# One more 1024-row block of output columns 256 to 511 transposed before it is normalised, in a fused matmul and batch norm

## The chip, the core and the metric

The kernel runs on one core of a Trainium2 chip. The metric is the device time of one execution in microseconds (us). A profile shows one execution: its span runs from the first to the last instruction, and the device time is a little longer than that. All times of events below are counted in us from the start of the span.

## The reference

```python
y = np.matmul(x, weight)                     # x: 16 x 512 x 1024, weight: 1024 x 768, float32
mean = np.mean(y, axis=(0, 1), keepdims=True)
var = np.var(y, axis=(0, 1), keepdims=True)
y_norm = (y - mean) / np.sqrt(var + eps)
return gamma * y_norm + beta                 # 8192 x 768 float32, 25.17 MB
```

The statistics of a column run over all 8192 rows, so no element of a column can be finished before the last product of that column is known. After that, the rest is one multiplication by a scale and one addition of a shift for each column.

## The kernel before, in words

The 8192 rows are 16 chunks of 512 (C = 16). The 768 columns are six tiles of 128 (nt = 0 to 5). x comes in through POOL's DMA queue with a cast to bf16, DVE transposes it, and TensorE (PE) multiplies.

**Two layouts.** Tiles 0 and 1 are computed with the rows of the output on the partitions ("in rows"; L500 to L516). They are finished by a DVE multiplication and an addition on POOL or DVE, and stored by L945. Tiles 2 to 5 are computed with the columns on the partitions ("in columns"; L562 to L584): scale and shift are then one number for each partition. ACT copies each finished PSUM bank to SBUF as bf16 (L714; tile 2 from chunk 4 on L719 and L723, which also sum), and DVE takes statistics (L710). Such a block has to be transposed before it is stored. A block is two chunks, 128x1024 (GY = 2), and its store is 512 KB.

**Three ways to finish a block in columns.** The tables MODE (L276) and RAW (L278) choose.
- "xact" (col_block, L1190): normalise in columns, on ACT for tile 2 (L1022) or on DVE for tile 3 (L1025); transpose by a DMA that SP issues (L1219); convert bf16 to float32 on ACT (L1231); store from SP (L1201).
- "pe" (the rest of tile 4): normalise, transpose on PE (L1043), copy out on ACT (L1209), store.
- "raw" (raw_turn, L1098, and raw_block, L1165): transpose the block by a DMA that SP issues, before any statistics are known, into a tile r_sb of the y pool (L1105). When scale and shift are known, raw_spread (L1126) lays them out along the free dimension (L1140 to L1157, in a PSUM bank). Then DVE multiplies (L1173, 128x1024), POOL adds (L1177), and SP stores (L1181).

Before the change tile 2 and tile 3 have blocks 0 and 2 raw (chunks 0, 1 and 2, 3), and their six other blocks "xact". Tile 4 has blocks 0, 2, 4, 6 raw.

**The order of the work.** Every operation is a Task with a due time, engines with costs, dependences and the memory slots it takes. arrange (L122) is a greedy planner: it goes through time and, on the engine that can begin first, places the ready task with the earliest due time (within 0.2 us). The resulting order on each engine is fixed in the program. A queue waits in order: an instruction whose input is late holds up everything behind it on its engine, SP included. Raw transposes of chunks 0 to 3 are entered with an early due time (L1121 to L1124); those of later chunks when all products of their tile are entered (L1275 to L1277). All raw transposes wait for the last load of x (gate, L1120). Of the raw blocks, raw_block number i (block 2i) is due at start + STEP * i + RAWDUE (L1284).

**Memory that the change touches.** The ring (RING, L279) is 6144 float32 words a partition. An "xact" block takes 1536 words of it when its transpose is issued (1024 until its store has landed); a raw block takes 1024 when its multiplication begins. The y pool has 29 tiles (YB). There are eight PSUM banks; the spread scale and shift of a tile hold one until its last raw block is multiplied.

**The tail.** Tile 5 is last. Its statistics close after the last product; then come a chain of small operations, DVE normalisation (L1347), PE transposes (L1043), ACT copies (L1360) and eleven stores (L1363). Before them one block of tile 4, held back for this, is stored (L1254).

Of the kernel before, what the change touches and what calls it, by code (L numbers as in the profile page):

```python
# [227 lines left out]
def kernel(  # L228
# [46 lines left out]
    PARTED, LATE, SINGLE = (4,5,7,8,9,10), (12,13,14,15), (2,3,6)  # L275
    MODE = {2:'xact',3:'xact',4:('pe',)*8}  # L276
    MODE = {nt: m if isinstance(m, tuple) else (m,) * (C // GY) for nt, m in MODE.items()}
    RAW, RAWADD, RAWDUE = {2:(0,2),3:(0,2),4:(0,2,4,6)}, {2:'POOL',3:'POOL',4:'POOL'}, {2:14.0,3:8.0,4:8.0}  # L278
    RING = 3 * CH // 32 * KQ // 2  # L279
    ENG = {"ACT": nc.scalar, "DVE": nc.vector, "POOL": nc.gpsimd, "SP": nc.sync}  # L280

# [1129 lines left out]
```

## Time and profile before

| | |
|---|---|
| time, median of 3 runs | 206.23 us (206.06 to 206.47) |
| the profiled execution: device time | 206.31 us |
| its span | 204.5 us |
| busy in the span: PE, DVE, ACT, POOL | 190.3, 159.2, 145.3, 128.3 us |
| HBM read, written | 36.71 MB, 25.17 MB |
| stores of blocks out of the ring, 512 KB | 37, 3.8 us to landing |
| transposes by DMA: "xact", raw | 12, 8 |

"Busy" counts the time in which an engine works on an instruction; a busy PE may still run matmuls that overlap. "To landing" is the time from the issue of a DMA to the arrival of its last byte. In the table by stretches, each engine has its busy time and, in brackets, the number of its instructions; then come the granted TensorE clock (1.00 is full), the busy share of the 16 DMA engines (packets of different queues overlap, so it goes over 1) and the GB/s that they moved.

### The profile page before, as it was taken

The numbers are of one execution on the slowest core, as the hardware profiler recorded it, in microseconds if no ns is written. First come the engines' busy times: TensorE is split into PE (matmuls) and PEld (weight loads), VectorE is DVE, ScalarE is ACT, GpSimd is POOL, SyncE is SP. The second block draws the span as 40 slices with busy tenths as digits, with TensorE's granted clock in tenths as the row PEclk, the third lists the DMA queues.
The fourth block names the chain that finished last, engine by engine and source line by source line (L and its number), as shares of the span: only waits on it lengthen the run. The fifth ranks groups of instructions, "written<-read, shape, count | busy, mean of one in ns | idle before, by whom it ended". The sixth has DMA issues, their size and how long they took to land.

```text
span 204.5 us, 3492 instructions
## 1 busy us (share of the span) xinstructions
PE 190.3 (93%) x1202; PEld 114.7 (56%) x1202; DVE 159.2 (78%) x248; ACT 145.3 (71%) x260; POOL 128.3 (63%) x152
## 2 busy tenths in 40 slices
PE   7999999999999999999999999999999999996800
PEld 3468555656588888777865444444444445445500
DVE  4031879999999999969988998977999787687700
ACT  2001361369989999998879766999998878936930
POOL 7877954877499989996303999389626402880000
PEclk9999999999999999999999999999999999999965
DMA  4999999999999999999599899999999999999996
GB/s 75 161 202 195 196 196 196 196 197 196 189 195 196 197 199 193 196 197 194 98 203 212 309 338 324 253 314 311 320 287 191 291 336 314 347 343 346 331 347 196
DMA packets 99602, 49.00 MB, mean 240 GB/s; under 512 B 25344, under 2 KB 99072, under 8 KB 99584
## 3 DMA queue, kind: packets, MB, share of 16 engines
q0 software_dynamic: 34624, 18.36, 65.2%
q1 hardware_dynamic: 64960, 30.42, 55.1%
q8 instruction: 9, 0.15, 0.3%
q14 instruction: 9, 0.07, 0.1%
HBM read 36.71 MB, written 25.17 MB: 303 GB/s over the span
## 4 chain that ended last, share of the span: by engine, by line
PE 76%; DMA 10%; ACT 4%; DVE 3%; POOL 2%; issue 1%; ACTq 0%; DVEq 0%; POOLq 0%
PE y_ps L574 49%; PE y_ps L509 21%; DMA w_sb<-in_weight_dram 6%; ACT o_sb L1360 3%; DMA ring<-in_x_dram 3%; PE y_ps L813 3%; DMA r_sb<-y_sb 1%; PE o_ps L1043 1%; POOL ring L402 1%; PE y_ps L752 1%; POOL w_sb L386 1%; DVE xT_sb L434 1%; DVE y_sb L1063 1%; ACTq L1406 0%; PE tot_ps L870 0%
## 5 line engine op out<-in xcount | busy, mean ns | idle before, releaser
L574 PEld LDWEIGHTS <-w_sb 128*128 128x128 bf16 x520 | 50.4, 97 | 57.4
L574 PE MATMUL y_ps<-xT_sb,w_sb 128*128 128x512 bf16 (+1 forms) x272 | 59.3, 371 | 0.0
L574 PE MATMUL y_ps<-x_pl,w_sb 128*128 128x512 bf16 x248 | 57.0, 379 | 0.0
L402 POOL DMA_DIRECT2D ring<-in_x_dram x76 | 47.3, 626 | 13.7 <-DVE xT_sb L427 5.0
L509 PE MATMUL y_ps<-w_sb,xT_sb 128*128 128x256 bf16 x448 | 50.5, 273 | 0.2 <-DVE xT_sb L434 0.2
L509 PEld LDWEIGHTS <-xT_sb 128*128 128x128 bf16 x448 | 43.7, 98 | 7.4 <-DVE xT_sb L434 0.8
L434 DVE STREAM_TRANSPOSE xT_sb<-ring 128x1024 f32<-128x1024 f32 (+1 forms) x29 | 31.2, 1111 | 13.3 <-DMA ring<-in_x_dram 13.2
L710 DVE BATCH_NORM_STATS2 stats<-y_ps 128x6 f32<-128x512 f32 x46 | 30.8, 686 | 6.8 <-PE y_ps L574 6.6
L546 ACT COPY x_pl<-xT_sb 128x1024 bf16<-128x1024 bf16 x34 | 34.8, 1059 | 1.7 <-DVE xT_sb L434 1.7
L714 ACT CAST y_sb<-y_ps 128x512 bf16<-128x512 f32 x51 | 28.5, 593 | 9.1 <-DVE stats L710 5.5
L941 POOL TENSOR_TENSOR ring<-ring,sum 128x1024 f32<-128x1024 f32 (+1 forms) x11 | 23.8, 2186 | 15.2 <-DVE ring L936 15.1
L658 ACT ACTIVATE sq_sb<-y_ps 128x512 f32<-128x512 f32 x28 | 16.5, 613 | 16.8 <-PE y_ps L509 16.4
L665 POOL TENSOR_TENSOR sum<-sum,sq_sb 128x512 f32<-128x512 f32 x20 | 25.5, 1276 | 3.4 <-ACT sq_sb L658 2.3
L661 DVE TENSOR_TENSOR sum<-y_ps,sum 128x512 f32<-128x512 f32 x28 | 18.9, 675 | 6.4 <-ACT sq_sb L658 5.4
L1177 POOL TENSOR_TENSOR ring<-ring,sum 128x1024 f32<-128x1024 f32 x8 | 19.5, 2448 | 5.7 <-issue 4.5
L671 ACT CAST y_sb<-y_ps 128x512 bf16<-128x512 f32 x28 | 16.0, 602 | 7.7 <-DVE sum L661 7.5
L936 DVE TENSOR_TENSOR ring<-y_sb,a_ps 128x1024 f32<-128x1024 bf16 (+1 forms) x16 | 16.7, 1079 | 0.3 <-DMA out_dram<-ring 0.3
L1144 POOL COPY sum<-sum 32x256 f32<-32x256 f32 (+1 forms) x17 | 5.3, 315 | 15.6 <-ACT sum L1144 8.8
L1231 ACT CAST ring<-ring 128x1024 f32<-128x1024 bf16 x12 | 12.7, 1060 | 2.3 <-DMA ring<-y_sb 2.3
L427 DVE STREAM_TRANSPOSE xT_sb<-ring 128x2048 bf16<-128x2048 bf16 x6 | 13.5, 2288 | 0.3 <-DMA ring<-in_x_dram 0.2
L1043 PE MATMUL o_ps<-ident,y_sb 128*128 128x128 bf16 x96 | 11.3, 221 | 1.6 <-DVE y_sb L1347 1.5
L590 PE MATMUL idle_ps<-idle_sb 128*128 128x512 f32 x18 | 11.2, 784 | 1.5 <-DVE idle_sb L316 1.5
(104 smaller groups left out, 152.4 us busy)
## 6 DMA issues: line engine op xcount, KB each, us to landing
out_dram<-ring SPq DMA_DIRECT2D x37, 512.0 KB, 3.8
ring<-in_x_dram POOLq DMA_DIRECT2D x52, 256.0 KB, 8.8
out_dram<-o_sb SPq DMA_DIRECT2D x6, 512.0 KB, 5.4
ring<-in_x_dram POOLq DMA_DIRECT2D x16, 128.0 KB, 6.0
w_sb<-in_weight_dram POOLq DMA_DIRECT2D x8, 192.0 KB, 6.1
out_dram<-ring SPq DMA_DIRECT2D x6, 256.0 KB, 3.6
ring<-in_x_dram POOLq DMA_DIRECT2D x4, 192.0 KB, 7.8
out_dram<-o_sb SPq DMA_DIRECT2D x3, 256.0 KB, 3.4
```

The costliest lines, as they stand in the source:

```text
L402: bi = seq(nc.gpsimd.dma_start(x_bf[32 * i:32 * i + 32], src[:, :, KQ * i:KQ * (i + 1)]))
L434: seq(nc.vector.transpose(dst, src[:, :, jw0:jw1]))
L509: seq(nc.tensor.matmul(y_ps[:, s], x_of(c, jw, e, t * P, (t + 1) * P), w_sb[:, jw, e, 0:NA], start=(s == 0 and jw == 0 and e == 0), stop=( ...
L546: seq(nc.scalar.copy(dst, pairs) if eng == "ACT" else ENG[eng].tensor_copy(dst, pairs))
L574: seq(nc.tensor.matmul(y_ps, w_sb[:, jw, e, nt * P:(nt + 1) * P], moving(c, jw, e, q0 * QR, q1 * QR, parted), start=(jw == 0 and e == 0 an ...
L661: seq(nc.vector.tensor_add(sum1, slot.tile[:, 0:n], sum1))
L665: seq(ENG[eng].tensor_add(acc, acc, state["sq"][:, 0:n]))
L710: seq(nc.vector.bn_stats(dst, slot.tile))
L714: seq(nc.scalar.copy(y(nt, c), slot.tile))
L936: seq(nc.vector.tensor_mul(slot.o, y_row[c].y[:, s0:s1], aff[0][:, None, :].to_broadcast([P, n, NA])))
L941: seq(ENG[eng].tensor_add(slot.o, slot.o, row[:, None, :].to_broadcast([P, n, NA])))
L1177: seq(ENG[eng].tensor_add(slot.o, slot.o, row[:, None, :].to_broadcast([P, n, P])))
```

## The change

Block 4 (chunks 4 and 5) of tile 2 and of tile 3 goes from "xact" to raw. Nothing else is edited; the planner arranges the whole program anew from the changed list of tasks.

```diff
-    RAW, RAWADD, RAWDUE = {2:(0,2),3:(0,2),4:(0,2,4,6)}, {2:'POOL',3:'POOL',4:'POOL'}, {2:14.0,3:8.0,4:8.0}
+    RAW, RAWADD, RAWDUE = {2:(0,2,4),3:(0,2,4),4:(0,2,4,6)}, {2:'POOL',3:'POOL',4:'POOL'}, {2:14.0,3:8.0,4:8.0}
```

## The prediction

> **What bounds the kernel now.** I read the waits of PE first, then the table by stretches, then SP's timeline and the landings of its stores.
>
> ```profile
> PE o_ps L1043 <- DVE y_sb L1347: 1.5, 1, 1.5
> PE idle_ps L590 <- DVE idle_sb L316: 1.5, 1, 1.5
> PE y_ps L509 <- DVE xT_sb L434: 0.2, 1, 0.2
> ```
>
> These are all of PE's waits: 1.5 us at the start, 0.2 us, and 1.5 us at the end, for the statistics of tile 5. From 110 to 186 PE never waits, and its starts follow each other at 0.216 or 0.226 us a matmul. So PE ends its last product at 186.15, and no edit that leaves the matmuls alone makes that earlier. The first store of tile 5 is issued at 188.85. What follows is 4.19 MB of stores.
>
> ```profile
> 116.00:136.00 20.00, 20.00 (x92) 8.67 (x91) 18.68 (x23) 16.32 (x39) 16.40 (x7) 1.00 0.90 292
> 136.00:152.00 16.00, 16.00 (x75) 7.20 (x74) 13.69 (x27) 15.96 (x24) 9.62 (x11) 1.00 1.15 323
> 152.00:160.00 8.00, 8.00 (x38) 3.60 (x37) 7.01 (x10) 6.16 (x9) 5.92 (x9) 1.00 1.25 193
> 160.00:173.00 13.00, 13.00 (x73) 6.29 (x71) 10.07 (x23) 11.44 (x22) 2.18 (x4) 1.00 1.19 327
> 173.00:186.00 13.00, 13.00 (x77) 6.84 (x76) 9.76 (x15) 8.38 (x13) 9.41 (x4) 1.00 1.15 344
> 186.00:190.00 4.00, 2.43 (x30) 1.55 (x28) 3.50 (x13) 3.15 (x9) 0.00 (x0) 1.00 1.15 346
> 190.00:204.50 14.50, 3.63 (x46) 2.47 (x44) 3.18 (x10) 6.21 (x8) 0.00 (x0) 0.69 0.96 289
> ```
>
> The last two columns are the reading. Stores alone run at 344 to 346 GB/s (173 to 190): that is a full queue, 1.51 us for a store of 512 KB. At 116 to 136 (292) and 152 to 160 (193) the queue is short of work or stuck; from 160 on it is full up to the end, but for a dip at 190 to 192 (308 GB/s). Look also at ACT: 15.96 of 16 us in 136 to 152. There ACT is what makes blocks ready.
>
> ```profile
> 180.40 5.01 SPq L1181 DMA_DIRECT2D out_dram<-ring  x3
> 187.07 1.04 SPq L1254 DMA_DIRECT2D out_dram<-ring  x2
> 188.85 11.01 SPq L1363 DMA_DIRECT2D out_dram<-o_sb  x11
> ```
>
> The last store of tile 4, issued at 184.34, lands at 190.00, the two of L1254 at 190.75 and 191.52, the first of tile 5 at 191.91, the last at 203.62. The landings follow each other at 1.51 us per 512 KB with no break, although the mean of the 16 engines dips at 190. So one engine is behind the others and stays so: after 202.3, where the rate breaks off, 34 or so packets of 27 ns follow, 0.92 us. The packet records show why that can be: an instruction fetch of 16 KB at 180.50 took 0.92 us. **The end is the backlog of the slowest DMA engine.** Were the queue empty when tile 5 comes, the end would be 0.9 us earlier and no more, because 188.85 is PE's.
>
> **The change, part by part.** For each of the two blocks:
>
> Removed. Tile 2: one normalisation on ACT (L1022, 1.25 us) and one conversion (L1231, 1.06): 2.31 us of ACT. Tile 3: one conversion, 1.06 us of ACT, and one DVE normalisation (L1025, 0.54). Two L1219 transposes, and 1536 words of ring each. ACT is full from 130 to 152, so there 2.31 us make the next blocks of tile 2 ready earlier: the first normalisation, at 127.24, is that of block 6 instead of 4, each later conversion comes one place sooner, and the last store of tile 2's columns (156.29) comes at about the place of the one before it (151.96).
>
> Added. Two DVE multiplications (L1173, 1.22 us each), two POOL additions (L1177, 2.35 to 2.80), two L1105 transposes, two stores: the same stores, from L1181 instead of L1201. DVE gains 2.44 - 0.54 = 1.90 us. It lies beside PE, which no DVE operation has held up so far. DVE is busy 13.69 of 16 us in 136 to 152, so the first multiplication (about 145, behind those at 139.39 and 142.20) fits, but statistics of tile 3 queue behind it. Without that room it costs up to 1.22 us on the chain of tile 3. POOL idles from 146.31 to 151.95 and from 161.00 to 169.76, with room for both additions.
>
> Moved. Transposes first. A transpose takes 0.92 us of a full queue: in 160 to 162 1023 of its packets go with 735 store packets, and 735 at the full rate of 678 per us need 1.08 of the 2 us. Block 4 of tile 2 is kept by ACT at 101, so its transpose can follow the other six, which SP issues from 99.55 to 107.64; it takes SP 1.25 us, to 108.9, ahead of the first store at 109.14. The queue has no stores then, so this place costs nothing but a start of the first stores up to 1.2 us later. Up to 136 the queue has room (share 0.90 against 1.07 to 1.15 when full), and ring space has shown no wait before 133. If ring space does run out there, DVE's stream of tiles 0 and 1 slips by up to 1.2 us. On the other side it gains 0.92 us where it was: I take 0 for the first and the gain for the second, since the 116 to 136 row is the nearest.
>
> Block 4 of tile 3 is kept at about 135; its transpose moves from 152.60 to 136 to 140. SP waits in order, so if the keep is late (ACT's L714 trail PE by 2 to 3 us there), the stores behind it wait, 0 to 1.4 us. I take 0, since ACT has become lighter.
>
> Tile 3's column blocks all move up one place. Before, their transposes stand at 152.60, 154.38, 161.65, 165.41, 168.08 and 170.04, the third held by the ring until the last store of tile 2 landed at 161.52. So the one at 170.04 goes, and 0.92 us of DMA work leaves the full stretch, and one store may leave the stretch after 173 too (1.51 us: before, two of tile 3's are issued after 173). The third raw store of tile 3 comes at about 164, after the third addition (161.0 to 163.4).
>
> The y pool gets r_sb of tile 2 from 107 to 147: at 107.7 I count 28 tiles in use of 29, so there is just room. For PSUM, the spread bank is held some 3 us longer; the longest wait of a finished bank for its ACT copy is 7.1 us (PE end 155.21, keep 162.27), about five of eight banks. No wait of PE: 0. A bank missing would cost PE up to 1.2 us directly.
>
> **Sum.** Backlog removed after 160: 0.92 us sure if the shift holds, up to 0.92 + 1.51 = 2.43. Cap at the end: 0.9 us. Against it: up to 1.22 us (DVE) and 1.2 us (start of the stores). The working value is 0.6 us, two thirds of the cap: of a freed 0.92 us I leave a third for a later third raw block. Span 204.5 - 0.6 = 203.9; with the 1.8 us around it (206.31 - 204.53), 205.7 us. The profiled execution stands 0.08 us above the median of the runs, which I neglect.
>
> **A rule of the skill against the change.** POOL's raw additions took 2.35 to 2.80 us, and the long one, within 141.14 to 146.31, lay beside a DVE copy at 143.34. The Trainium skill, "SBUF — State Buffer", section "SBUF: two separate sides", says that VectorE in a two-port mode and GpSimd exclude each other on a shared port pair for a whole instruction. The 2.80 agrees with it; no row here shows the lock itself.
>
> **Rivals.**
> 1. Slower. The new addition on POOL, 2.35 us at about 146.3 to 148.7, falls on DVE's copies and first normalisation of tile 3 (147.24 to 149.77), and the new multiplication delays tile 3's statistics by 1.22 us; the same again at 161.0 to 163.4, where three normalisations stand (161.12 to 162.57). Tile 3's stores come late. At 169 to 171 the queue is nearly dry (a store issued at 169.42 lands in 3.3 us, the shortest of L945 in 2.8), so 0.5 us of lateness are absorbed and the rest goes into the end. Of 1.22 to 2.35 us I take 1.7 less 0.5: 207.5. It decides when tile 3's column stores are more than 0.5 us later than before. For it: DVE is close to full from 140 to 150. Against it: normalisation to transpose has 3 to 4.8 us of room there (147.77 to 152.60). That rule of the Trainium skill is this rival's mechanism, by its wording, and it would give the same 207.5.
> 2. No change. The work leaves the queue before 160 but is given back: stores are limited by tile 4's POOL chain (last addition ends at 184.31), so the backlog at 185 stays. 206.2. For it: four additions in a row from 173.67, with little idle time between. Against it: DVE's multiplication at 175.15 waited 1.0 us for a store to land.
> 3. The change doesn't do what it says: the planner reorders more than the two blocks, or the late tile of the y pool or bank stalls PE. 207 to 208, by 1 to 2 us of PE.
>
> **How the numbers follow.** Forecast with its spread (205.3 to 205.8): 0.43. Rival 2: 0.23. Rival 1: 0.26. Rival 3: 0.08. About 0.2% (0.4 us) is what a measurement of this kernel can tell from no change. So faster 0.43, same 0.23, slower 0.34. The low end is the cap, 206.2 - 0.9 = 205.3; the high end, 207.6, takes in rival 1 and leaves out its worst and most of rival 3.
>
> **What would show it.** Right: 20 transposes in all as before, but seven L1105 issues before the first store; the last store of tile 2's columns near 152; GB/s in 152 to 160 above 193; a deeper dip at 186 to 191; landings of tile 5 breaking the even 1.51 us. Wrong: PE waits between 110 and 186, L1219's last issue not before 169, or stores of tile 4 landing after 190.0.

## The result and the profile after

The changed kernel takes 207.25 us (median of 8 runs, 206.70 to 207.72), the kernel before 206.11 us beside it (8 runs). The ratio on record is 1.0039, with a 95% interval of 1.0023 to 1.0055 (the two medians alone would give 1.0055). It is slower, by some 0.8 us (0.5 to 1.1), where 0.5 us faster was forecast.

The profiled execution of the changed kernel has a device time of 207.64 us and a span of 205.9. Not all of its 1.3 us more of span is the change. I split each execution at three events of PE and SP. PE's first operation at L870 (99.11 in before) comes when all loads that PE waits for have landed; what lies ahead of it varies by chance, and here it is 99.95. From there on there are three terms: **PE** (L870 to the end of the last product, L752), **chain** (from there to the issue of tile 5's first store, L1363) and **tail** (from there to the last landing).

| | PE | chain | tail |
|---|---|---|---|
| before | 87.04 | 2.70 | 14.77 |
| after | 87.05 | 2.69 | 15.25 |
| after, a second execution | 87.05 | 2.70 | 15.27 |

PE and the chain are as they were. All of the loss that the profile shows is in the tail, the stores of tile 5: 0.49 us. So what the forecast wanted to shorten, the backlog of the queue, became longer.

The table by stretches of the changed kernel, with the columns as before (the last two are the DMA share and the GB/s):

```profile
116.00:136.00 20.00, 20.00 (x92) 8.62 (x91) 18.82 (x22) 16.35 (x42) 16.56 (x8) 1.00 0.97 320
136.00:152.00 16.00, 16.00 (x75) 7.18 (x74) 13.84 (x23) 14.85 (x25) 7.88 (x5) 1.00 1.16 320
152.00:160.00 8.00, 8.00 (x38) 3.60 (x37) 7.86 (x16) 7.45 (x16) 2.29 (x2) 1.00 1.18 258
160.00:173.00 13.00, 13.00 (x66) 6.06 (x64) 12.72 (x27) 9.97 (x19) 7.75 (x5) 1.00 1.05 286
173.00:186.00 13.00, 13.00 (x80) 6.76 (x78) 9.98 (x15) 9.06 (x15) 8.76 (x6) 1.00 1.06 316
```

Up to 160 the queue does more than before: 320 instead of 292 GB/s, and 258 instead of 193 in 152 to 160. After 160 it does less: 286 instead of 327, then 316 instead of 344. The lead is earned and given back. Look at DVE in 160 to 173: 12.72 of 13 us, where it was 10.07.

The packets say how much. I count each packet of SP's queue at what it takes in a full queue (0.92 us for the 1024 of a transpose, 1.51 for the 1024 of a 512 KB store of tiles 2 to 5, and 1.36 for 512 KB of the row stores of tiles 0 and 1, which both kernels have), and line the executions up at L870:

| us of full queue done by | 128 | 152 | 160 | 172 | 176 | 186 |
|---|---|---|---|---|---|---|
| before | 20.4 | 41.6 | 46.5 | 58.5 | 62.5 | 72.4 |
| after | 21.3 | 42.4 | 48.5 | 59.0 | 62.0 | 71.8 |
| after, the second execution | 21.3 | 42.1 | 48.7 | 59.4 | 62.0 | 71.8 |

At 160 the changed kernel is 2.0 to 2.2 us of transfers ahead; at 176 it is 0.5 behind and stays so. In before the queue loses nothing between 160 and 186. In after it runs dry for 1.3 to 1.5 us in 160 to 164 and for 1.0 to 1.4 in 172 to 176, 2.6 to 2.8 us together. 0.6 us more is left to do at 186, and the tail is 0.5 us longer.

SP's timeline of the changed kernel (start, length, line, number of DMAs) shows the second dry place:

```profile
165.84 2.37 SPq L1219 DMA_TRANSPOSE ring<-y_sb  x1
168.26 0.57 SPq L1181 DMA_DIRECT2D out_dram<-ring  x1
168.94 3.16 SPq L1219 DMA_TRANSPOSE ring<-y_sb  x2
173.31 6.89 SPq L1201 DMA_DIRECT2D out_dram<-ring  x6
180.39 7.36 SPq L1181 DMA_DIRECT2D out_dram<-ring  x4
187.92 1.45 SPq L1254 DMA_DIRECT2D out_dram<-ring  x2
```

Between 168.26 and 173.31 no store is issued. Before, stores came at 169.42 and from 171.77 on, and the first raw store of tile 4 at 176.32; now all four raw stores of tile 4 stand at the end, after 180, and the last lands at 191.32 instead of 190.00. (All events of this execution are 0.84 us late by the load phase; differences below are given less that.) SP's waits in 156 to 178, first in before, then in after (total us, times, longest), tell what it stood for:

```profile
SPq L1201 <- ACT ring L1231: 1.6, 2, 1.0
SPq L1201 <- ACT ring L1209: 0.9, 1, 0.9
```

```profile
SPq L1181 <- POOL ring L1177: 2.7, 2, 1.5
SPq L1201 <- ACT ring L1231: 2.2, 3, 1.1
SPq L1201 <- ACT ring L1209: 1.4, 1, 1.4
```

In after SP stands for POOL's raw additions ahead of the stores at 162.28 and 164.59, 1.5 and 1.25 us, which it does not in before; this is the first dry place. It stands for ACT ahead of the stores at 173.31 and 175.13; this is the second. (The view also puts 6.2 us down to tile 3's normalisations, L1219 <- L1025. That is the time SP spends on issuing the transposes themselves, 1.26 us each at least: those at 155.24, 165.84, 168.94 and 170.79 begin within 0.3 us of the end of the instruction before them, and the normalisations for the last three had ended at 164.93, 167.76 and 168.20.)

ACT's timeline, in before and in after, shows what the store at 173.31 waits for:

```profile
168.63 1.00 ACT L1144 COPY sum<-sum 32x64 f32<-32x64 f32 x4
170.70 1.04 ACT L1231 CAST ring<-ring 128x1024 f32<-128x1024 bf16 x1
```

```profile
171.21 1.00 ACT L1144 COPY sum<-sum 32x64 f32<-32x64 f32 x4
172.24 1.05 ACT L1231 CAST ring<-ring 128x1024 f32<-128x1024 bf16 x1
```

The conversion (L1231) of this block of tile 3 stands behind the spread of tile 4's scale (L1144). DVE has the input of that spread ready (L1141) from 168.32 on in before and from 170.89 on in after, 1.7 us later when lined up. In before the conversion follows the landing of its transposed block (170.38) by 0.3 us; in after the block has landed at 170.76 and waits 1.5 us.

The additions and normalisations of tile 3 are late too, though SP hardly waits for a normalisation. DVE's timeline has tile 3's normalisations, in before and then in after (the line L995 is the one-column scale):

```profile
147.24 0.53 DVE L1025 TENSOR_SCALAR y_sb<-y_sb,scale,shift 128x1024 bf16<-128x1024 bf16 x1
150.89 0.54 DVE L1025 TENSOR_SCALAR y_sb<-y_sb,scale,shift 128x1024 bf16<-128x1024 bf16 x1
155.90 0.54 DVE L1025 TENSOR_SCALAR y_sb<-y_sb,scale,shift 128x1024 bf16<-128x1024 bf16 x1
161.12 1.45 DVE L1025 TENSOR_SCALAR y_sb<-y_sb,scale,shift 128x1024 bf16<-128x1024 bf16 x3
```

```profile
148.22 2.27 DVE L995 TENSOR_TENSOR scale<-rstd,gamma_sb 128x1 f32<-128x1 f32 x1
...
154.67 0.53 DVE L1025 TENSOR_SCALAR y_sb<-y_sb,scale,shift 128x1024 bf16<-128x1024 bf16 x1
156.95 0.54 DVE L1025 TENSOR_SCALAR y_sb<-y_sb,scale,shift 128x1024 bf16<-128x1024 bf16 x1
164.40 0.53 DVE L1025 TENSOR_SCALAR y_sb<-y_sb,scale,shift 128x1024 bf16<-128x1024 bf16 x1
167.22 0.98 DVE L1025 TENSOR_SCALAR y_sb<-y_sb,scale,shift 128x1024 bf16<-128x1024 bf16 x2
```

The first came at 147.24 and comes at 154.67, 6.6 us later; the last three came from 161.12 on, one behind the other, and come at 164.40, 167.22 and 167.7, 2.4 to 4.8 us later. POOL's raw additions of tile 3, in before and in after:

```profile
156.12 4.88 POOL L1177 TENSOR_TENSOR ring<-ring,sum 128x1024 f32<-128x1024 f32 x2 [1.81 <-issue]
```

```profile
159.90 7.24 POOL L1177 TENSOR_TENSOR ring<-ring,sum 128x1024 f32<-128x1024 f32 x3 [5.71 <-DVE ring L1173]
```

In before the three normalisations follow the second addition (156.12 + 4.88 = 161.00). In after two of them follow the third (159.90 + 7.24 = 167.14). That is the planner's order: arrange keeps a normalisation of DVE and an addition of POOL apart (L159 to L165 and L212 to L213, "port"). And the additions begin 2.9 us later: POOL waits for the multiplication (L1173), which needs the spread of the scale. The planner has moved that spread from POOL to ACT for tiles 2 and 3 (L1144), but from DVE's L1141 to the multiplication it takes 3.2 us, as before (3.1): it is DVE that begins it 2.9 us later.

### The profile page after: what moved, and what is told of

Read it like the earlier page. It is cut to its first block, busy times and chain, and to the rows that moved or that the text cites. A ratio compares the mean times of both kernels' runs of the same rounds, so it can differ in the third digit from the quotient of the medians.

```text
span 205.9 us, 3489 instructions
## 1 busy us (share of the span) xinstructions
PE 189.1 (92%) x1202; PEld 114.0 (55%) x1202; DVE 162.8 (79%) x251; ACT 144.7 (70%) x269; POOL 128.6 (62%) x140
## 4 chain that ended last, share of the span: by engine, by line
PE 76%; DMA 9%; ACT 4%; DVE 3%; POOL 2%; issue 1%; ACTq 0%; DVEq 0%; POOLq 0%
PE y_ps L574 48%; PE y_ps L509 21%; DMA w_sb<-in_weight_dram 6%; PE y_ps L813 4%; DMA ring<-in_x_dram 3%; ACT o_sb L1360 3%; PE o_ps L1043 1%; POOL ring L402 1%; PE y_ps L752 1%; POOL w_sb L386 1%; DVE xT_sb L434 1%; DVE y_sb L1063 1%; ACTq L1406 0%; PE tot_ps L870 0%; DVE ring L941 0%
## 5 line engine op out<-in xcount | busy, mean ns | idle before, releaser
L1177 POOL TENSOR_TENSOR ring<-ring,sum 128x1024 f32<-128x1024 f32 x10 | 23.7, 2393 | 18.0 <-DVE ring L1173 11.3
L710 DVE BATCH_NORM_STATS2 stats<-y_ps 128x6 f32<-128x512 f32 x46 | 30.4, 683 | 5.1 <-PE y_ps L574 4.9
L546 ACT COPY x_pl<-xT_sb 128x1024 bf16<-128x1024 bf16 x32 | 32.7, 1059 | 1.7 <-DVE xT_sb L434 1.7
L1173 DVE TENSOR_TENSOR ring<-r_sb,a_ps 128x1024 f32<-128x1024 bf16 x10 | 11.9, 1209 | 0.4 <-DMA out_dram<-ring 0.3
L590 PE MATMUL idle_ps<-idle_sb 128*128 128x512 f32 x18 | 9.6, 684 | 1.5 <-DVE idle_sb L316 1.5
L1231 ACT CAST ring<-ring 128x1024 f32<-128x1024 bf16 x10 | 10.4, 1051 | 0.0
```

The source lines that it names most:

```text
L546: seq(nc.scalar.copy(dst, pairs) if eng == "ACT" else ENG[eng].tensor_copy(dst, pairs))
L710: seq(nc.vector.bn_stats(dst, slot.tile))
L1177: seq(ENG[eng].tensor_add(slot.o, slot.o, row[:, None, :].to_broadcast([P, n, P])))
```

## The experiments

My theory after the profile is **supply**: from 160 on the end is set by when the blocks of tiles 3 and 4 are ready, and a lead that the queue gains earlier is not kept. Its rivals: the **queue** (the prediction's: work that leaves it early is missing at the end), the **port** (POOL's third addition locks DVE out), the **start** (a later load phase), and the **late raw stores** of tile 4 as the backlog. The expectations below stand as they were written at the time.

In all of them the ratio is to the kernel before, run beside on the same chip, with its 95% interval. The terms are those of the profiled execution, as differences from before, and "timed" is the ratio's difference at 206.2 us.

| run | PE | chain | tail | sum | ratio | timed |
|---|---|---|---|---|---|---|
| same | 0.01 | 0.00 | -0.02 | -0.01 | 0.9993 (0.9975 to 1.0012) | -0.1 |
| after | 0.01 | 0.00 | 0.48 | 0.49 | 1.0039 (1.0023 to 1.0055) | 0.8 |
| again | 0.01 | 0.00 | 0.50 | 0.50 | 1.0037 (1.0022 to 1.0051) | 0.8 |
| t2only | 0.00 | 0.87 | -0.17 | 0.70 | 1.0034 (1.0015 to 1.0054) | 0.7 |
| t3only | 0.55 | 0.00 | 0.54 | 1.09 | 1.0043 (1.0025 to 1.0061) | 0.9 |
| oneinput | 0.01 | 0.00 | 0.50 | 0.51 | 1.0042 (1.0026 to 1.0057) | 0.9 |
| before_skip | -0.01 | 0.00 | -0.94 | -0.94 | 0.9970 (0.9953 to 0.9988) | -0.6 |
| after_skip | 0.01 | 0.00 | -0.94 | -0.92 | 0.9968 (0.9952 to 0.9983) | -0.7 |
| due4_2 | 0.00 | 0.20 | 1.15 | 1.36 | 1.0090 (1.0068 to 1.0112) | 1.9 |
| three4 | 0.44 | 0.00 | 0.93 | 1.37 | 1.0074 (1.0050 to 1.0098) | 1.5 |
| late3 | 0.81 | 1.57 | -0.14 | 2.25 | 1.0107 (1.0085 to 1.0129) | 2.2 |
| late3_one | 0.01 | 1.55 | -0.13 | 1.43 | 1.0058 (1.0038 to 1.0078) | 1.2 |
| free3 | 6.14 | 0.00 | -0.76 | 5.38 | 1.0305 (1.0276 to 1.0335) | 6.3 |
| free3_before | 0.00 | 0.00 | -0.36 | -0.35 | 1.0003 (0.9984 to 1.0022) | 0.1 |
| poolspread | 1.61 | 0.00 | 0.38 | 1.98 | 1.0087 (1.0058 to 1.0116) | 1.8 |
| t2due10 | 0.00 | 1.05 | -0.11 | 0.95 | 1.0062 (1.0040 to 1.0085) | 1.3 |
| before_lead | 0.01 | 0.00 | -0.52 | -0.51 | 0.9978 (0.9964 to 0.9992) | -0.5 |
| after_lead | 0.00 | 0.00 | 0.50 | 0.50 | 1.0045 (1.0028 to 1.0062) | 0.9 |

The sum goes with the timed difference to within 0.5 us in all runs but free3 (0.9), so the three terms may be used to say where a variant loses. For the changed program itself (after, again, oneinput, after_lead) the timed difference is 0.3 to 0.4 us above the profile's 0.5 in all four; where this rest lies stays open.

**again and same** are the two kernels once more, unaltered.

> The changed kernel once more, unaltered. Port-and-planner theory (the loss is made between 140 and 190: tile 3's scale waits for POOL, tile 4's raw blocks come late, the queue of stores is backed up when tile 5 comes): 207.2, and in the profile the last product of PE again at a place set by the load phase alone, with the last store of tile 4 issued some 0 to 0.5 us after PE's last product and a first landing of tile 5 about 3.5 us after its issue. Start theory (the loss is the 0.85 us by which PE was late from 26 us on in the first profile of the changed kernel): this profile shows it again, 0.7 to 1.0 us of lateness of PE at 26 us; if PE is on time there (25.6) and the device time is still 207, this theory falls.

> The kernel before, unaltered, for a second profile and as a control of the comparison: ratio 1.000. Start theory (part of the measured difference is that PE is later in the changed kernels from the load phase on): PE's last product here at 185.8 to 186.2, against 186.2 to 187.0 in the three profiles of changed kernels with the same order of PE. Chance theory: anywhere from 185.9 to 187.0, and the times around it spread as wide as those of the changed kernel.

again gave 207.19 us, same 206.40. The difference belongs to the program. L870 came at 99.27 and 99.80: a late load phase, which the first profile of the changed kernel suggested as a cause, comes to both kernels by chance.

**before_skip and after_skip: what is an empty queue worth?** Two raw stores of tile 4 (blocks 4 and 6) are left out, so their rows are not written.

```diff
         def store(eng):
+            if nt == 4 and c in (4, 6):
+                return
```

> The kernel before, with two of the 48 or so output stores left out: those of tile 4's raw blocks 4 and 6 (the work on them is done, in the same order). That takes 3.0 us of transfers out of the queue just ahead of tile 5. The prediction's theory (the end is the backlog of the slowest DMA engine, 0.9 us can be had): 205.2 to 205.4. The other reading, from the run with tile 2's block alone, where the last landing followed the first issue of tile 5 by 14.60 us in place of 14.77: the queue is as good as empty already, and the time falls by 0.2 us or less: 206.0.

> The changed kernel with the same two stores left out. Backlog theory (what the change costs is a queue that is 0.5 us fuller when tile 5 comes): it loses 0.5 us at least against the changed kernel (206.6 or less) and the last landing follows the first issue of tile 5 by 14.6 us in place of 15.26; if the backlog is all, it ends level with the kernel before under the same cut. If 0.3 us or more remain between the two cut kernels, something else is part of the loss, and PE's last product shows whether it is PE.

205.88 and 205.68 us. With 3.0 us less to store right ahead of tile 5, both have the same tail, 13.83 us, 0.94 less than before. This is the cap of the prediction (0.9 us), and by the tail it holds; timed, the two gain 0.6 and 0.7 us on the kernel before.

**t2only and t3only: half of the change each.**

```diff
-    RAW, ... = {2:(0,2,4),3:(0,2,4),4:(0,2,4,6)}, ...
+    RAW, ... = {2:(0,2,4),3:(0,2),4:(0,2,4,6)}, ...       # t2only
+    RAW, ... = {2:(0,2),3:(0,2,4),4:(0,2,4,6)}, ...       # t3only
```

> Only block 4 of tile 2 goes raw; tile 3 stays as before the change. If tile 2's third addition on POOL, beside tile 3's statistics, is the cause: 206.7 to 207.3, with a long wait of the one-column multiplication that makes tile 3's scale. If tile 3's block is the cause: 206.1. Start theory: 206.1 to 207.2 by chance, with the profile's lateness at 26 us equal to that of the device time.

> Only block 4 of tile 3 goes raw; tile 2 stays as before the change. If tile 2's block is the cause: 206.1, and no long one-column multiplication. If tile 3's block is the cause (its third addition lies before tile 4's spread and raw blocks): 206.7 to 207.3, with tile 4's last raw store 1 to 3 us later than 184.3 against PE's last product at 186.15.

207.13 and 207.28 us: each half costs as much as the whole, by something else each. In t2only DVE's last multiplication of a raw block waits 0.99 us for a store to land, to have ring space (183.32), and the last statistics of tile 5 stand behind it on DVE: the chain is 0.87 us longer. In t3only PE loses 0.55 us at 169.6 to 170.4, where it waits for a normalisation of tile 4 (L1025), and the tail is as in after.

**oneinput: the port.** In after the scale of tile 3, one column of 128 numbers, took 2.27 us beside a POOL addition (148.12 to 150.47), and 0.16 in before. Here the three one-column operations take one tensor input instead of two, the other as a scalar of each partition, in the same order.

```diff
-            seq(nc.vector.tensor_mul(scale[:, one], rstd, gamma_sb[:, one]))
+            seq(nc.vector.tensor_scalar(scale[:, one], rstd, gamma_sb[:, one], None, op0=ALU.mult))
```

> The changed kernel, in which three one-column DVE operations that make scale and shift of tiles 3 and 4 take one tensor and numbers of a partition in place of two tensors; the planner's order is the same, instruction for instruction. Port theory (the 2.27 us of tile 3's scale at 148.22 is a wait for POOL's addition, 148.12 to 150.47, because both read two tensors through a shared port): that operation takes 0.1 to 0.3 us, tile 3's first normalisation comes up to 2.1 us earlier than 154.67, and the time falls to 206.3 to 206.9. If it is not what sets the end: 207.2, though the wait is gone. If it is no port at all: the 2.27 us stays.

DVE's timeline and POOL's:

```profile
147.09 0.21 DVE L995 TENSOR_SCALAR scale<-rstd,gamma_sb 128x1 f32<-128x1 f32 x1
```

```profile
146.94 4.70 POOL L1177 TENSOR_TENSOR ring<-ring,sum 128x1024 f32<-128x1024 f32 x2 [0.50 <-DMA out_dram<-ring]
```

Beside an addition all the same, it takes 0.21 us. The Trainium skill, "SBUF — State Buffer", section "SBUF: two separate sides", says that a DVE instruction with two SBUF inputs and a GpSimd instruction that reads SBUF shut each other out for a whole instruction; the 2.27 and the 0.21 agree with it. But the time is 207.27 us, and the tail 15.27: the 2 us are not on the way to the end. Two statistics operations of DVE (L710, at 150.15 and 151.88) stand ahead of the first normalisation and now wait 0.33 and 1.03 us for PE, so that it comes at 153.09 instead of 153.60 in again.

**due4_2 and three4: the late raw blocks of tile 4.** They stand at the end of SP's queue, so they might be the backlog. due4_2 makes them due 6 us earlier, three4 makes the last of them "pe" again.

```diff
-    ... RAWDUE = ... {2:14.0,3:8.0,4:8.0}
+    ... RAWDUE = ... {2:14.0,3:8.0,4:2.0}                  # due4_2
-    RAW, ... = {2:(0,2,4),3:(0,2,4),4:(0,2,4,6)}, ...
+    RAW, ... = {2:(0,2,4),3:(0,2,4),4:(0,2,4)}, ...        # three4
```

> The changed kernel with the due time of tile 4's raw blocks set 6 us earlier (2.0 in place of 8.0): the planner's order is the same until tile 4 is finished; then the spread and the first raw multiplication come before two statistics in place of behind them, and the four raw stores go among tile 4's others, not all last. If the late raw blocks of tile 4 make the backlog: last raw store of tile 4 issued 1.5 to 2.5 us earlier against PE, the tail 14.6 to 14.9, time 206.6 to 206.8. If the backlog comes from the gaps of the queue before 176: no change, 207.2.

> The changed kernel with tile 4's raw block 6 given back to PE (tile 4 has three raw blocks in place of four, so that POOL's raw additions are nine in all, one more than before). If the chain of four additions on POOL (177.28 to 186.63, back to back) sets the last stores of tile 4 and with them the backlog: last raw store issued 2.4 us earlier, tail 14.8 or less, 206.4 to 206.8. If the gaps before 176 set it: no gain, 207.2.

208.37 and 208.18 us, worse by 1 us. In both the queue loses more ahead of 176 (1.8 and 1.9 us in 172 to 176, where after and again lose 1.0 and 1.4) and is at 71.2 and 70.4 at 186, against 71.8 in after (three4 needs one transpose less, so its 70.4 compare as 71.3). So the late place of the raw stores is not shown to cost anything: with fewer or earlier ones the queue is dry for longer and the time is longer.

**late3, late3_one, free3: the normalisations of tile 3.** late3 makes the third raw block of tile 3 due 8 us later, so that the normalisations come ahead of its addition.

```diff
-                raw_block(nt, GY * i, start + STEP[nt] * i + RAWDUE[nt])
+                raw_block(nt, GY * i, start + STEP[nt] * i + RAWDUE[nt] + (8.0 if (nt, i) == (3, 2) else 0.0))
```

> The changed kernel with the due time of tile 3's third raw block (the one that the change adds) set 8 us later: DVE's last three normalisations of tile 3 come ahead of its multiplication in place of behind it. Theory of the gaps (the queue of stores, ahead by 2 us of work at 160, runs dry at 160 to 164 and at 172 to 176, because the third raw block of tile 3 holds tile 3's last normalisations back from 161.6 to 166.9): the last normalisation comes 2 to 4 us earlier, SP waits less for L1025 than the 3.5 us of the changed kernel, the two gaps, 2.7 us together, shrink by 1 us or more, and the tail from first issue to last landing falls from 15.26 to 14.8 or less: 206.4 to 206.8. Theory of supply (tile 4's stores can't be ready earlier, whatever tile 3 does): the gaps move but their sum stays, 207.2.

The last three normalisations come at 161.23, 163.48 and 164.2, some 3 us earlier than in after, and the time is 208.95 us, above both expectations. DVE's timeline shows what took their place:

```profile
167.54 2.27 DVE L995 TENSOR_TENSOR scale<-rstd,gamma_sb 128x1 f32<-128x1 f32 x1
...
185.24 1.22 DVE L1173 TENSOR_TENSOR ring<-r_sb,a_ps 128x1024 f32<-128x1024 bf16 x1 [2.36 <-DMA out_dram<-ring]
186.37 0.69 DVE L710 BATCH_NORM_STATS2 stats<-y_ps 128x6 f32<-128x512 f32 x1
```

The late addition (167.45) now holds the scale of tile 4, and PE loses 0.8 us; and DVE waits 2.36 us for ring space at 185.24, ahead of tile 5's statistics, which makes the chain 1.57 us longer. late3_one is late3 with the operations of oneinput:

> The kernel of the run late3 (the changed kernel with the due time of tile 3's third raw block 8 us later), and the one-column operations L992, L995 and L996 with one tensor input instead of two, in the same order on every engine. In late3 the normalisations of tile 3 came 2 to 3 us earlier, but L995 of tile 4 took 2.27 us beside a POOL addition, PE then waited 0.8 us, and the time was 208.95. Theory S (the queue runs dry at 160 to 164 and 172 to 176 because tile 3's and tile 4's blocks are not ready; the lock did not make those gaps): the lock goes, L995 takes 0.2 us, PE's wait of 0.8 us at 172.8 gets shorter or goes, and the time falls by 0.3 to 0.8 us from 208.95 to 208.1 to 208.7, but stays above the changed kernel's 207.2, because the last raw blocks still wait for ring space ahead of the last statistics. Theory L (the lock is what spoils it): all of the 1.7 us come back, 207.0 to 207.3 or less. Where neither holds the time stays within 0.2 us of 208.95.

207.83 us: 1.1 us come back. The scale takes 0.21 us, PE's wait is gone (the PE term 0.01), and the chain is as much longer as in late3 (1.55). That is a little more than was expected of the lock alone (208.1 to 208.7) and clearly less than all. Here, other than in oneinput, the lock had a price of 0.8 us of PE.

free3 takes the planner's rule away: normalisations of tile 3 may stand beside POOL's additions. free3_before is the same edit in before.

```diff
-        a = task(due, ..., norm(nt, c, GY), [fin_task] + keeps, nt > GA, uses=[yslot])
+        a = task(due, ..., norm(nt, c, GY), [fin_task] + keeps, nt > GA + 1, uses=[yslot])
```

> The changed kernel, in which the planner no longer keeps tile 3's normalisations apart from POOL's additions (nothing else is edited): all five normalisations of tile 3 come earlier in DVE's order. Theory of the gaps: as for late3, with the first stores of tile 3 earlier too: 206.2 to 206.8. Port theory (the chip keeps them apart anyway): normalisations of up to 2.9 us beside POOL's additions, or additions of up to 2.9 us, and no gain, 207.2 or more.

> The same edit of the planner in the kernel before, as the control of free3: SP's and POOL's orders stay as they are, only DVE's normalisations of tile 3 move. The queue is full from 160 on in the kernel before, so earlier normalisations have nothing to fill: 206.2 to 206.5, no change. If it gains 0.3 us or more, a gain of free3 says nothing of the change.

213.09 and 206.64 us. DVE's timeline of free3:

```profile
162.23 1.68 DVE L1025 TENSOR_SCALAR y_sb<-y_sb,scale,shift 128x1024 bf16<-128x1024 bf16 x1
164.44 1.96 DVE L1025 TENSOR_SCALAR y_sb<-y_sb,scale,shift 128x1024 bf16<-128x1024 bf16 x1
...
172.32 2.26 DVE L995 TENSOR_TENSOR scale<-rstd,gamma_sb 128x1 f32<-128x1 f32 x1
```

A normalisation beside an addition takes 1.68 and 1.96 us instead of 0.53. The two begin 2 to 3 us earlier than in after, and the last three end 0.1 to 1.3 us earlier (163.9, 166.4 and 168.1 instead of 164.9, 167.7 and 168.2). Tile 4's scale comes 4 us later, beside another addition, and PE waits 4.3 us for the normalisation behind it:

```profile
PE o_ps L1043 <- DVE y_sb L1025: 4.3, 1, 4.3
```

So the planner's rule is worth its price here.

**poolspread: the spread back on POOL.** As in before, where POOL did it for tiles 2 and 3.

```diff
-        g = task(now, {"POOL": (0.8, 0.85), "ACT": (0.9, 1.0)}, gather, [d])
-        s = task(now, {"POOL": (1.2, 1.25), "ACT": (1.0, 1.1)}, deal, [g])
+        g = task(now, {"POOL": (0.8, 0.85)} if nt < 4 else {"ACT": (0.9, 1.0)}, gather, [d])
+        s = task(now, {"POOL": (1.2, 1.25)}, deal, [g])
```

> The changed kernel with the spread of scale and shift of tiles 2 and 3 (L1144, seven copies each) held on POOL as in the kernel before, where the planner had moved them to ACT, and that of tile 4 on ACT. Theory S: what is short is the readiness of tile 3's blocks at 160 to 164, and its chain runs over POOL's additions. The spread costs POOL some 2.5 us a tile ahead of those additions, so tile 3's additions and last normalisations come no earlier, the gap in the queue at 160 to 164 stays at 1 us or more, and the time is within 0.4 us of the changed kernel's 207.2. Rival (the move of the spread to ACT delayed the blocks, since ACT converts them): ACT is lighter by 2.3 us at 140 and again at 156, the conversions of tile 3 come earlier, the gaps close, and the time falls to 206.2 to 206.6.

208.40 us, more than either theory had. Tile 3's additions come at 162.92 to 172.2, 3 to 5 us later than in after, the queue loses 3.1 us in 152 to 160, and PE waits 1.4 us for tile 4. From L1141 to the first multiplication the spread takes 6.2 us here instead of 3.2. So the move of the spread to ACT did not cause the loss.

**t2due10: tile 2's block alone, without its longer chain.** t2only with tile 4's raw blocks due 2 us later, to take the multiplication away from ahead of the last statistics.

```diff
-    ... RAWDUE = ... {2:14.0,3:8.0,4:8.0}
+    ... RAWDUE = ... {2:14.0,3:8.0,4:10.0}
```

> Only tile 2 has its third raw block (the run t2only, 207.13, ratio 1.0034), and tile 4's raw blocks are due 2 us later (RAWDUE of tile 4 is 10.0 instead of 8.0), which puts one statistics operation of tile 5 ahead of the second of tile 4's multiplications and takes the column stores of tile 4 ahead of its second raw store. In t2only a multiplication that waited for ring space stood ahead of the last statistics, and the chain from PE's last product to tile 5's first store was 3.56 us instead of 2.70; from that store on t2only needed 14.60 us against 14.77 in the kernel before. Theory S (what t2only loses is this chain alone): the chain returns to 2.7 to 2.9 us and the time to 206.1 to 206.4, no different from the kernel before, or up to 0.2 us below it. Rival (the backlog in the queue is what t2only loses too): the chain may shorten, but the tail grows to 15.0 us or more, and the time stays at 206.9 to 207.3.

207.95 us: a miss of both expectations. The chain is 3.75 us: another multiplication, at 184.06, stands late ahead of the statistics. It did not part the two theories.

**before_lead and after_lead: the lead alone.** Two stores of tile 2's columns (chunks 8 to 11; in before issued at 143.06 and 146.38) are left out, so their rows are not written. It takes 3.0 us out of the queue before 152, and leaves the readiness of every later block alone.

```diff
         def store(eng):
+            if nt == 2 and c in (8, 10):
+                return
             seq(ENG[eng].dma_start(dst(), slot.o))
```

> The kernel before, with the stores of two column blocks of tile 2 (chunks 8, 9 and 10, 11) left out, so that these rows are not written; everything else keeps its place and order. It takes 3.0 us of work out of the queue before 152 and nothing out of what comes later: a lead by itself, with the readiness of tile 3's and tile 4's blocks as it was. Theory S (from 160 on the end is set by when the blocks of tiles 3 and 4 are ready, so a lead gained earlier is not kept): the queue runs dry somewhere in 160 to 176, the tail from tile 5's first store stays at 14.5 us or more, and the ratio to the kernel before is 0.998 to 1.001. Rival Q (the reckoning of the prediction: work that leaves the queue early is missing at the end, up to the cap): the tail falls to 13.8 to 14.1 us, and the ratio is 0.996 to 0.997, as in before_skip, where the two stores left out were late ones.

> The changed kernel with the same two stores of tile 2 left out (chunks 8 to 11 of its columns are not written). Theory S: the lead at 160 grows to 3 us or more, the gaps at 160 to 164 and 172 to 176 grow by as much, and the time stays within 0.3 us of the changed kernel's (ratio to the kernel before 1.002 to 1.005, tail 15.0 us or more). Rival Q: the tail falls by 0.5 to 1.4 us and the ratio is 0.997 to 1.000.

206.18 us (0.9978) and 207.28 us (1.0045). Work done, with the 3.0 us that were left out added, so that the rows compare:

| us of full queue done by | 160 | 172 | 176 | 186 | tail |
|---|---|---|---|---|---|
| before | 46.5 | 58.5 | 62.5 | 72.4 | 14.77 |
| before_lead, + 3.0 | 48.4 | 59.7 | 62.9 | 72.8 | 14.24 |
| after | 48.5 | 59.0 | 62.0 | 71.8 | 15.25 |
| after_lead, + 3.0 | 48.9 | 59.4 | 61.9 | 71.8 | 15.27 |

The tables by stretches, of before_lead and then of after_lead:

```profile
160.00:173.00 13.00, 13.00 (x71) 6.31 (x70) 9.67 (x23) 10.19 (x20) 2.56 (x4) 1.00 1.07 291
173.00:186.00 13.00, 13.00 (x76) 6.72 (x74) 10.02 (x15) 8.37 (x13) 9.37 (x4) 1.00 1.14 343
```

```profile
160.00:173.00 13.00, 13.00 (x67) 6.13 (x66) 11.97 (x26) 9.54 (x19) 7.28 (x6) 1.00 1.01 278
173.00:186.00 13.00, 13.00 (x81) 6.92 (x79) 10.33 (x15) 9.05 (x14) 8.80 (x5) 1.00 1.06 318
```

This is what the other runs could not part. In the changed kernel 3.0 us less of early work give nothing at all: the tail is the same to 0.02 us, and so is the work done by 186. In the kernel before they give 0.5 of 3.0 us; its queue, full from 160 on (327 GB/s), now falls to 291 in 160 to 173. Both expectations were too sharp for before_lead: the tail lies between the two, and the ratio at the edge of the one that a lead is not kept.

The traces show where the changed order takes a lead away. after, again, oneinput, after_skip and after_lead have the order of the changed kernel and are 2.0 to 2.9 us ahead of before at 160 (after_lead with its 3.0 us added), but at 176 all five have done 61.9 to 62.0 us of work. In all five, lined up, a statistics operation of DVE (L710) begins at 169.14 to 169.16, when PE's product is there; behind it come L1141 at 170.04 or 170.05, the spread on ACT, and the conversion of tile 3's block at 171.38 to 171.40, although the block landed at any time from 169.14 to 169.92. So the end of the second dry place is tied to PE's pace by the order on DVE and ACT, and the first dry place, which differs from run to run, does not reach the end.

## Why the prediction was wrong

- **What bounds the kernel: half right.** PE never waits between 110 and 186 and ends its product 87.05 us after L870, as before. The cap was right: 0.9 forecast, 0.94 measured with an empty queue.
- **"From 160 on it is full up to the end" was the reading that failed.** I took a full queue for the bound. It was full, but with little in store: the blocks became ready just as the queue came to them. before_lead shows it, with 0.5 us of 3.0 kept.
- **The step that failed** is the one on the moved column blocks: "So the one at 170.04 goes, and 0.92 us of DMA work leaves the full stretch", entered as sure and worth 0.6 us. One transpose did go, but work that leaves the queue is not time that leaves it. The last transpose is issued at 170.79, not before 169, behind raw stores for which SP waited 2.7 us on POOL's additions; and the conversion behind it on ACT waits for tile 4's spread. In place of 0.92 us less, the queue ran dry twice, 2.6 to 2.8 us together. The balance: 2.0 to 2.2 us ahead at 160, 2.6 to 2.8 us lost after it, 0.6 us behind at 186; forecast -0.6, measured +0.5 us in the tail.
- **The steps up to 160 were right.** Seven L1105 transposes stand ahead of the first store (110.03), tile 2's last column store comes at 151.53 (152 forecast), and 152 to 160 moves 258 GB/s (above 193). None of it reaches the end.
- **"DVE gains 1.90 us. It lies beside PE" was right for PE and wrong for the rest.** PE did not wait, but DVE is busy 12.72 of 13 us in 160 to 173. It has the input of tile 4's spread ready 1.7 us later (L1141), ACT's conversion stands behind that spread, and so the queue waited in PE's stead. The sum names up to 1.22 us of DVE on tile 3's chain and has no term for tile 4's. I priced the third addition by whether POOL has room, which it has, and not by what the order puts behind it.
- **Rival 1 came nearest, by chance**, with 207.5 for a measured 207.25. The normalisations of tile 3 are late as it says, by 2.4 to 6.6 us and not 1.7, its last three column stores come 0.7, 2.2 and 0.3 us later (lined up), and a lead of 2 us, which I had not entered there, takes up much of it. But SP hardly waits for them. Its lock is seen (2.27 us on the scale, 1.7 to 2.0 on a normalisation in free3), but in the changed kernel it costs the end nothing (oneinput). What holds the stores is the order: POOL's additions, and tile 4's spread ahead of tile 3's conversion.
- **The two costs that I set to nothing** (a later start of the stores, the y pool and the bank) cost nothing: the first store comes at 110.03 instead of 109.14, 0.8 us of this from the load phase, with no loss behind it up to 160, and PE has no wait.
- **What stays open.** Shown is that the end of the changed kernel is set by the readiness of tiles 3 and 4 and not by the amount of work ahead of them, and where in the order of ACT and DVE the queue last runs dry. Not shown is that another order there would give the time back: the lock, the spread of tiles 2 and 3, the place of the raw stores and that of the third addition were each changed, and none gave time back, but no run moved tile 3's conversion ahead of tile 4's spread. And the 0.3 us between the profile's 0.5 and the timed 0.8 have no place yet.

## What to carry to other kernels

A queue that is full is not yet the bound: see whether there is a ready block behind the one that is being sent, and if not, work taken out of the queue turns into idle time, as 2.5 of 3.0 us did here. When work moves from one engine to two others, price not only the room on them but also what the new order keeps waiting (here stores behind additions, and a conversion behind another tile's spread). To learn whether a lead is worth anything, leave out as much work early and once as much late: 3.0 us early gave 0.5 us of the tail in the kernel before and nothing in the changed one, 3.0 us late gave 0.9 and 1.4 us and left both with the same tail. And check a wait that a view names against the timeline: 6.2 us of "waiting" were the issue of transposes.

## What the runs showed of the hardware

- A DVE operation on one column takes 0.16 us alone and 2.27 beside a POOL addition when both its inputs are tensors, 0.21 when one is a scalar of the partition. A normalisation of 128x1024 takes 0.53 us alone, and 1.6 to 2.0 beside an addition in free3.
- The load phase ends by chance at 99.1 to 100.3 (PE's L870) in all kernels of this program, some 1 us of difference between two executions: more than the change makes. Differences of 0.5 us are better read from events behind it.
